# Folding a norm's channel factors into the two operations that split a weight, block by block

## The chip, the cores and the metric

The kernel runs on one core of a Trainium2 chip. The metric is the time of one execution in microseconds on the device. Engines are named as in the profile: PE is TensorE (PEld its weight loads), DVE is VectorE, ACT is ScalarE, POOL is GpSimd, and SP is SyncE, whose queue here issues all transfers between HBM and the core's memory.

## The reference

A trunk of two layers over 1024 positions and 1024 channels, float32 throughout. The first layer is a Conformer convolution: RMS norm, a projection to 3072 columns (two halves of a gated unit and an output gate), a causal depthwise convolution with 31 taps, layer norm, SiLU, gate, output projection, norm, residual. The second is differential attention with 8 heads over keys and values from the residual stream after the first layer. What matters here are its projections, each of which reads a normalised stream:

```python
def _rms_norm(x, g):
    y = xf * lax.rsqrt(jnp.mean(xf * xf, axis=-1, keepdims=True) + EPS)
    return (y * g.astype(jnp.float32)).astype(x.dtype)

kvh = _rms_norm(x, kv_g) @ w_kv        # keys and values, 2048 columns
h = _rms_norm(x, g_pre)
u = h @ w_in                           # queries and output gate, 2048 columns
```

The norm's factor per position is applied to a product after the matmul; its factor per channel, `kv_g` or `b_g_pre`, belongs to a row of the weight and can be multiplied into it.

## The kernel before, in words

**Products.** PE multiplies in a reduced float32 format. Every operand is therefore kept as a high part (the rounded value) and a low part (the rest), and each product is three matmuls: high by high, high by low, low by high (`THREE`). `act[t]` holds the split stream of one half of the positions (512 columns, t = 0 or 1), channels on the partitions, in eight blocks of 128 channels.

**Weights.** A weight piece is 128 output columns of a projection: a tile `wraw` of 128 partitions x 1024 elements, which are 8 channel blocks of 128 columns. `wprep` loads it (L564 is the line of every DMA), ACT rounds it into the high half of a tile `whl` (`R.copy`, L532) and DVE subtracts to give the low half (`R.tt`, L539). There are two `wraw` and three `whl` tiles (and one more, `whx`, for the first query piece). 32 of the pieces, those of the second layer's keys, values, queries and gate, carry a norm's channel factors: `wprep` gets them as `gain`. A value piece (`vproj`) is 4 channel blocks of 256 columns, two pieces for two heads; the other 24 (`zbproj`, `heads`) are 8 blocks of 128 columns. The factors lie in `pr` (`kv_g`, `b_g_pre`) or, for queries, in an 8-column tile `sm8`, which the profile lists as `sm`. In the kernel before, one DVE multiplication over the whole tile puts the factors into `wraw` in place ahead of the split.

**Stages.** The first layer (gated unit, convolution by DVE for four channel blocks and by PE for the other four, gate, layer norm, output projection, residual) fills about the first 430 us. Then the attention's heads follow, until about 960 us: for each head its weight pieces, projections (`pj`), scores (`s`, L1152), a softmax numerator (`e`: DVE L1161, then ACT L521), transposes (`t`, L1204), the split of the transposed weights (`at`: ACT L532, DVE L539), products with the values (`o`), and a norm over the head (`finish`). The next head's pieces are prepared while one head's attention runs. The output projection ends the kernel.

**Order.** Nothing runs in program order. The program records each instruction with its data dependences into a plan; `Plan.schedule` then simulates the five engines with a price in nanoseconds per instruction (`alts`), and puts every instruction at its place in its engine's queue, by a priority made of its place in the program, the longest chain behind it, constants (`TUNE`) and an offset for each labelled group (`OFFSETS`; "w" at a label's end is its weight piece, "cv0" the first channel block's convolution, "s23" the third pair of scores of head 3). Each engine then runs its queue in that order. An instruction whose input isn't there holds all behind it on that engine.

Of the kernel before, what the change touches and what calls it, by code (L numbers as in the profile page):

```python
# [12 lines left out]
AF = mybir.ActivationFunctionType  # L13
ALU = mybir.AluOpType
# [4 lines left out]
P = 128  # L19
# [111 lines left out]
class Op:  # L131
# [13 lines left out]

TUNE = dict(LOOK=2.2803,
           BG=19323277573972505648901158565292249389628248258332383962132468097051787264,
           FS=45301, FS0=1201, CS=0, EV=157158, WT=0.8342, CV0=46679, CV1=113660, WP=2955,  # L150
           ZS=-61794, PT0=8, PT1=8)

OFFSETS = {"": 20890, "w": 8673, "start1": -150, "x0": 332, "x1": 403, "x2": 60, "x3": 48533,
# [55 lines left out]


class Clock:
# [24 lines left out]
class Plan:  # L236
# [53 lines left out]
    def schedule(self):  # L290
# [16 lines left out]
        for o in self.ops:  # L307
            o.prio = max(o.seq + o.shift + OFFSETS.get(o.label, 0), min(o.seq, o.floor))
            o.prio = TUNE["WT"] * -tail[o] / 200.0 + (1 - TUNE["WT"]) * o.prio
            if o.early:  # L310
# [43 lines left out]
        while done < len(self.ops):  # L354
            best = None
            for e in engines:
# [22 lines left out]
                if pick is not None:  # L379
                    lim = s + TUNE["LOOK"] * dict(pick.alts)[e]  # L380
                    least = pick.prio - TUNE["BG"]
                    rush = [(t, o.prio, o) for t, o in cand
# [186 lines left out]
def trunk(ctx: ExitStack, tc, xT, wC, prm, wA, wAo, wK, wV, wB, wBo, wBo2, gpost, outT, out2):  # L569
# [3 lines left out]
    R = Plan(nc)  # L573
# [82 lines left out]
    f = lambda v: v.bitcast(F32)  # L656
# [8 lines left out]
    def wprep(src, gain=None, n_k=NT, k0=0, tag="whl", lo=("DVE",), parts=1):  # L665
        w = S // n_k
        sh, R.shift = R.shift, R.shift - TUNE["WP"]
        lb, R.label = R.label, R.label + "w"
        wl = "W" if R.lane in "BF" and tag == "whl" else R.lane
        hl = R.tile(tag, 2, n_k, w, lane=wl)  # L670
        raw = R.tile("wraw", n_k, w, lane=wl)
        n = n_k // parts
        for a in range(0, n_k, n):
            ks = slice(a, a + n)
            R.dma(raw[:, ks], src.rearrange("p (k c) -> p k c", c=w)[:, ks], 4 * P * S // parts,
                  R.gate)
            if gain is not None:
                g = gain[0][:, gain[1] + k0 : gain[1] + k0 + n_k].bc(2, [P, n_k, w])
                R.tt(raw.all(), raw.all(), g, ALU.mult)
            R.copy(hl[:, 0, ks], raw[:, ks])  # L680
            hl.done = R.tt(hl[:, 1, ks], raw[:, ks], f(hl[:, 0, ks]), ALU.subtract, lo)
        R.shift, R.label = sh, lb
        return hl
# [757 lines left out]
```

## Time and profile before

| what | value |
|---|---|
| runs shown, median | 1124.56 us (three runs, 1121.05 to 1125.19) |
| the profiled execution | 1127.16 us, span of its instructions 1125.4 us |
| mean granted clock of PE | 0.981 of full speed |
| busy: PE, DVE, ACT | 1074.9 us, 899.9 us, 445.6 us |

Busy times are sums of the instructions' durations, overlaps counted once. The span is from the first to the last instruction of the profiled execution; that execution lies 2.6 us above the median of the runs shown.

### The profile page before, as it was taken

The page shows a single profiled execution, that of the slowest core. Times are in us where ns is not written, and L with a number is a line of the kernel's source. Part 1 is how long each engine was busy: PE and PEld are TensorE (multiplying, and loading weights), DVE is VectorE, ACT ScalarE, POOL GpSimd, SP SyncE. Part 2 cuts the span into 40 slices and gives each one's busy share as a digit, 9 for nine tenths or more (in the row PEclk, how much of TensorE's full clock was granted, in tenths as well). Part 3 has the DMA queues.
Part 4 walks back from the last instruction along what each step waited for, and adds up shares of the span by engine and source line. Part 5 has one row for each costly group of instructions (what it writes and reads, how often), then busy time and mean ns, then how long its engine had stood idle before and what let it go on. Part 6 is the DMA issues. An engine that isn't in the chain of part 4 may idle for free.

```text
span 1125.4 us, 15385 instructions
## 1 busy us (share of the span) xinstructions
PE 1074.9 (96%) x5790; PEld 883.0 (78%) x5790; DVE 899.9 (80%) x1812; ACT 445.6 (40%) x824; POOL 4.8 (0%) x19
## 2 busy tenths in 40 slices
PE   7999899998999998999999999999999999999996
PEld 5788788886888886886888887988888888767874
DVE  7999969989895389938778778787886966878566
ACT  8112021125465354434345334454443443455421
POOL 0000000000000001000000000000000000000000
PEclk9999899998999999999999999999999999989998
DMA  9121541172112354441114121232121311731293
GB/s 339 63 75 57 169 150 65 48 244 55 57 38 73 100 169 146 168 169 38 38 63 145 58 75 38 76 131 75 58 75 58 113 57 38 262 106 60 96 328 141
DMA packets 52409, 121.31 MB, mean 108 GB/s; under 512 B 5488, under 2 KB 22128, under 8 KB 51184
## 3 DMA queue, kind: packets, MB, share of 16 engines
q1 hardware_dynamic: 52336, 120.34, 31.3%
q8 instruction: 45, 0.74, 0.3%
q14 instruction: 28, 0.23, 0.1%
HBM read 90.96 MB, written 29.36 MB: 107 GB/s over the span
## 4 chain that ended last, share of the span: by engine, by line
PE 79%; DVE 8%; DMA 7%; ACT 3%; issue 2%; SPq 1%; DVEq 0%; ACTq 0%
PE pj L498 45%; PE pjA L498 11%; PE pjB L498 6%; PE o L498 6%; PE s L1152 6%; PE t L1204 3%; DMA wc<-wC 2%; PE pjC L498 1%; DMA wraw<-wBo 1%; SPq L564 1%; DVE ya L559 1%; PE t L498 1%; DMA wraw<-wK 1%; ACT tmp L521 1%; DVE msum L539 1%
## 5 line engine op out<-in xcount | busy, mean ns | idle before, releaser
L498 PE MATMUL pj<-act,whl 128*128 128x512 f32 x1968 | 537.4, 405 | 7.0 <-ACT whl L532 5.7
L498 PEld LDWEIGHTS pj<-act,whl 128*128 128x128 f32 x1968 | 358.0, 191 | 87.5 <-ACT whl L532 5.9
L498 PE MATMUL pjA<-act,whl 128*128 128x512 f32 x672 | 186.8, 402 | 0.6 <-DVE whl L539 0.6
L532 ACT CAST whl<-wraw 128x1024 fp32r<-128x1024 f32 (+1 forms) x84 | 86.0, 1027 | 174.9 <-PE pj L498 114.9
L498 PEld LDWEIGHTS pjA<-act,whl 128*128 128x128 f32 x672 | 127.3, 191 | 32.0 <-DVE whl L539 1.0
L559 DVE SCALAR_TENSOR_TENSOR ya<-cc,pr,ya 128x1024 f32<-128x1024 f32 x116 | 148.7, 1282 | 2.4
L521 ACT ACTIVATE e<-e,sm 128x128 f32<-128x128 f32 (+7 forms) x128 | 99.3, 777 | 99.6 <-DVE sm L1161 61.8
L539 DVE TENSOR_TENSOR whl<-wraw,whl 128x1024 fp32r<-128x1024 f32 (+1 forms) x84 | 100.2, 1195 | 32.9 <-ACT whl L532 32.7
L498 PE MATMUL pj<-whl,act 128*128 128x256 f32 x768 | 112.2, 284 | 3.4 <-DVE tmp L559 3.4
L498 PEld LDWEIGHTS pj<-whl,act 128*128 128x128 f32 x768 | 100.7, 189 | 7.3 <-DVE tmp L559 4.3
L498 PE MATMUL o<-at,vt 128*128 128x256 f32 x480 | 100.5, 299 | 0.7 <-ACT at L532 0.7
L1161 DVE CUSTOM_DVE_ANT_0 e<-s,dist 128x128 f32<-128x128 f32 (+7 forms) x128 | 94.6, 752 | 6.6 <-PE s L1152 4.1
L498 PEld LDWEIGHTS o<-at,vt 128*128 128x128 f32 x480 | 78.3, 189 | 14.7 <-issue 4.4
L539 DVE TENSOR_TENSOR at<-t,at 128x512 fp32r<-128x512 f32 (+1 forms) x80 | 50.7, 634 | 33.4 <-ACT at L532 31.2
L1152 PE MATMUL s<-ks,qs 64*128 64x512 f32 (+2 forms) x576 | 73.1, 372 | 2.6 <-DVE sm L1161 2.5
L532 ACT CAST at<-t 128x512 fp32r<-128x512 f32 (+1 forms) x80 | 43.4, 543 | 78.6 <-PE t L1204 74.9
L1152 PEld LDWEIGHTS s<-ks,qs 64*128 64x128 f32 x576 | 48.5, 187 | 23.5 <-issue 8.1
L559 DVE SCALAR_TENSOR_TENSOR e<-e,sm,e 128x128 f32<-128x128 f32 (+3 forms) x64 | 52.2, 816 | 1.4
L1204 PE MATMUL t<-ident,e 128*128 128x128 f32 x288 | 50.4, 275 | 2.6 <-DVE og L539 1.7
L539 DVE TENSOR_TENSOR tmp<-pj,rn 128x512 f32<-128x512 f32 x48 | 32.9, 688 | 24.5 <-PE pj L498 20.7
L498 PE MATMUL pjB<-act,whl 128*128 128x512 f32 x192 | 52.3, 397 | 0.0
L498 PEld LDWEIGHTS pjB<-xq,wc 128*128 128x128 f32 x320 | 39.8, 200 | 8.3 <-issue 7.2
(177 smaller groups left out, 1078.0 us busy)
## 6 DMA issues: line engine op xcount, KB each, us to landing
wraw<-wA SPq DMA_DIRECT2D x22, 512.0 KB, 3.5
wc<-wC SPq DMA_DIRECT2D x8, 1280.0 KB, 8.7
wraw<-wAo SPq DMA_DIRECT2D x16, 512.0 KB, 3.6
wraw<-wB SPq DMA_DIRECT2D x16, 512.0 KB, 3.5
v_d<-tmp SPq DMA_DIRECT2D x32, 256.0 KB, 2.7
vt<-v_d SPq DMA_DIRECT2D x16, 512.0 KB, 3.3
wraw<-wBo SPq DMA_DIRECT2D x16, 512.0 KB, 4.3
go_d<-fx SPq DMA_DIRECT2D x12, 512.0 KB, 2.6
```

The source lines that it names most:

```text
L498: e.matmul(w[0], lhsT=r[2 * i], rhs=r[2 * i + 1], start=start and i == 0, stop=stop and i == k - 1)
L521: e.activation(w[0], r[0], func, **kw)
L532: (e.copy if hasattr(e, "activation") else e.tensor_copy)(w[0], r[0])
L539: lambda e, r, w: e.tensor_tensor(w[0], r[0], r[1], alu), [a, b], [out])
L559: e.scalar_tensor_tensor(w[0], r[0], s if imm else r[2], r[1], o1, o2)
L564: return self.op([("SP", 475.0)], lambda e, r, w: e.dma_start(w[0], r[0]), [src], [out], nbytes, gate)
L1152: en.matmul(w_[2 * (m // 6) + m % 2], lhsT=r[2 * m], rhs=r[2 * m + 1], start=m % 6 < 2, stop=m % 6 >= 4)
L1161: en.tensor_tensor_reduce(w_[0], r[0], r[1], -(0.5 ** (h + 1)), 3e38, ALU.add, ALU.min, w_[1])
L1204: R.op([("PE", 110.0)], lambda en, r, w: en.transpose(w[0], r[0], ident), [aw[qq][:, k0 : k0 + P]], [t_ps[:, i, :]])
```

## The change: what it does, and the diff

Where `wprep` gets channel factors, the multiplication over the whole tile, the rounding over the whole tile and the subtraction over the whole tile go. In their place each channel block gets two instructions: ACT copies the block times its factor (one number per partition, taken from memory as the instruction's scale) into the high half, and DVE computes block times factor minus high half (`R.stt`) into the low half. `wraw` is no longer written. The plan's prices are set to 370 ns and 310 ns for each block, whatever its width. Pieces without factors are prepared as before.

All constants of `TUNE` that are shown in the diff and nearly all of `OFFSETS` have other values as well, so that every engine's queue may have another order in all stages. Of the offsets a few stand here.

```diff
-TUNE = dict(LOOK=2.2803,
-           BG=19323277573972505648901158565292249389628248258332383962132468097051787264,
-           FS=45301, FS0=1201, CS=0, EV=157158, WT=0.8342, CV0=46679, CV1=113660, WP=2955,
+TUNE = dict(LOOK=4.0183,
+           BG=4782923213790355517589053156738505591805890650812152609421540987954733536182410412032,
+           FS=45301, FS0=1201, CS=0, EV=157158, WT=0.7858, CV0=46679, CV1=113660, WP=2955,
...
-           "x4": 9275, "x5": 3939, "x6": -3452, "x7": 989, "w0": 9002, "ab00": -15021, "ab10":
-           39455, "cv0": 379, "w1w": 3465, "ab11": 1145, "cv1": 13614, "w2": -413, "ab12": 7686,
+           "x5": 16654, "x6": -974, "x7": 937, "w0": -2620, "ab00": 1963, "ab10": 27502, "cv0":
+           -21992, "w1w": 9710, "ab01": 10765, "ab11": -17917, "cv1": 33686, "w2w": 1053, "w2":
...
             if gain is not None:
-                g = gain[0][:, gain[1] + k0 : gain[1] + k0 + n_k].bc(2, [P, n_k, w])
-                R.tt(raw.all(), raw.all(), g, ALU.mult)
+                for k in range(a, a + n):
+                    g = gain[0][:, gain[1] + k0 + k : gain[1] + k0 + k + 1]
+                    R.act(hl[:, 0, k], raw[:, k], AF.Copy, scale=g).alts = [("ACT", 370.0)]
+                    hl.done = R.stt(hl[:, 1, k], raw[:, k], g, f(hl[:, 0, k]), ALU.mult,
+                                    ALU.subtract)
+                    hl.done.alts = [("DVE", 310.0)]
+                continue
             R.copy(hl[:, 0, ks], raw[:, ks])
             hl.done = R.tt(hl[:, 1, ks], raw[:, ks], f(hl[:, 0, ks]), ALU.subtract, lo)
```

## Rows read from the trace of the kernel before

**Rows 1.** The page's first part: busy time, share of span, instructions by engine.

```profile
PE 1074.9 (96%) x5790; PEld 883.0 (78%) x5790; DVE 899.9 (80%) x1812; ACT 445.6 (40%) x824; POOL 4.8 (0%) x19
```

**Rows 2.** Busy time by stretch: start:end, length, engines, granted clock, DMA.

```profile
0.00:430.00 430.00, 409.44 (x1889) 333.03 (x1890) 363.35 (x492) 156.39 (x247) 1.77 (x17) 0.98 0.35 116
...
430.00:960.00 530.00, 518.31 (x3161) 432.08 (x3159) 416.42 (x1011) 225.12 (x462) 2.99 (x2) 0.99 0.24 82
...
960.00:1125.00 165.00, 147.11 (x746) 117.86 (x742) 120.13 (x310) 64.14 (x115) 0.00 (x0) 0.94 0.48 169
```

**Rows 3.** The chain of waits, 425 to 520 us: start, length, engine, tile, line.

```profile
430.90 1.24 DVE wraw L539
...
459.36 0.87 DVE wraw L539
...
499.14 8.26 DMA wraw<-wK
```

**Rows 4.** Two stretches of the attention's start, columns as in rows 2.

```profile
430.00:466.00 36.00, 29.92 (x175) 24.86 (x173) 34.08 (x70) 13.76 (x23) 2.99 (x2) 0.95 0.34 116
...
430.00:520.00 90.00, 80.89 (x457) 66.13 (x456) 65.22 (x145) 37.08 (x68) 2.99 (x2) 0.96 0.39 133
```

**Rows 5.** Instructions in order of time near 507 us: start, length, [idle before].

```profile
507.43 1.23 DVE L539 TENSOR_TENSOR wraw<-wraw,pr 128x1024 f32<-128x1024 f32 x1 [2.69 <-DMA wraw<-wK]
...
508.92 0.71 PE L1152 MATMUL s<-ks,qs 64*128 64x256 f32 x5 [2.02 <-DVE sm L1161]
```

**Rows 6.** Groups by shape: busy us, mean ns of one, idle before.

```profile
L532 ACT CAST whl<-wraw 128x1024 fp32r<-128x1024 f32 x80 | 83.6, 1048 | 174.9 <-PE pj L498 114.9 <-PE pjA L498 21.0 <-issue 19.5
...
L539 DVE TENSOR_TENSOR whl<-wraw,whl 128x1024 fp32r<-128x1024 f32 x80 | 97.5, 1220 | 32.6 <-ACT whl L532 32.4
...
L539 DVE TENSOR_TENSOR wraw<-wraw,pr 128x1024 f32<-128x1024 f32 x24 | 29.3, 1220 | 5.5 <-DMA wraw<-wK 3.0 <-DMA wraw<-wV 2.5
...
L539 DVE TENSOR_TENSOR wraw<-wraw,sm 128x1024 f32<-128x1024 f32 x8 | 9.7, 1218 | 3.2 <-DMA wraw<-wB 3.2
...
L559 DVE SCALAR_TENSOR_TENSOR tmp<-pj,rt,tmp 128x256 fp32r<-128x256 f32 x32 | 13.9, 478 | 6.5 <-ACT tmp L521 4.3 <-DMA x1t_d<-xr 2.2
...
L521 ACT ACTIVATE e<-e,sm 128x256 f32<-128x256 f32 x16 | 8.1, 506 | 7.3 <-DVE sm L1161 7.3
...
L521 ACT ACTIVATE e<-e,sm 128x128 f32<-128x128 f32 x16 | 6.4, 402 | 14.5 <-DVE sm L1161 10.0 <-DVE sm L539 3.1 <-DVE sm L559 1.2
...
L559 DVE SCALAR_TENSOR_TENSOR e<-e,sm,e 128x128 f32<-128x128 f32 x8 | 2.8, 350 | 0.1
```

**Rows 7.** Instructions in order of time, runs of equal ones merged.

```profile
403.61 2.36 DVE L539 TENSOR_TENSOR whl<-wraw,whl 128x1024 fp32r<-128x1024 f32 x2
...
512.10 0.35 DVE L559 SCALAR_TENSOR_TENSOR e<-e,sm,e 128x128 f32<-128x128 f32 x1
512.37 1.22 DVE L539 TENSOR_TENSOR whl<-wraw,whl 128x1024 fp32r<-128x1024 f32 x1
...
461.61 0.88 DVE L559 SCALAR_TENSOR_TENSOR tmp<-pj,rt,tmp 128x256 fp32r<-128x256 f32 x2
...
115.04 2.26 ACT L521 ACTIVATE yq<-pjB,pr 128x128 f32<-128x128 f32 x8 [2.49 <-PE pjB L498]
```

**Rows 8.** Who waited for whom, PE alone: us, times, longest.

```profile
PE pjB L498 <- DMA xq<-ca_d: 6.4, 2, 5.0
...
PE pjB L498 <- DVE msum L539: 5.2, 1, 5.2
...
PE o L498 <- ACT at L532: 0.7, 1, 0.7
...
PE pj L498 <- ACT whx L532: 0.3, 1, 0.3
```

**Rows 9.** Two joints of the first layer, columns as in rows 2.

```profile
116.00:136.00 20.00, 15.00 (x66) 11.90 (x65) 19.43 (x17) 1.30 (x5) 0.25 (x2) 0.95 0.71 224
258.00:276.00 18.00, 12.80 (x46) 9.22 (x45) 18.00 (x26) 9.30 (x12) 0.00 (x0) 0.81 0.17 59
```

More of the change, by code (lines that the diff above doesn't have):

```diff
@@ L144 @@
            ("SP", "POOL"): 940.0, ("SP", "SP"): 1000.0}
-TUNE = dict(LOOK=2.2803,
-           BG=19323277573972505648901158565292249389628248258332383962132468097051787264,
-           FS=45301, FS0=1201, CS=0, EV=157158, WT=0.8342, CV0=46679, CV1=113660, WP=2955,
+TUNE = dict(LOOK=4.0183,
+           BG=4782923213790355517589053156738505591805890650812152609421540987954733536182410412032,
+           FS=45301, FS0=1201, CS=0, EV=157158, WT=0.7858, CV0=46679, CV1=113660, WP=2955,
            ZS=-61794, PT0=8, PT1=8)
-OFFSETS = {"": 20890, "w": 8673, "start1": -150, "x0": 332, "x1": 403, "x2": 60, "x3": 48533,
[55 rows of a table removed]
+OFFSETS = {"": 16772, "w": -7524, "x0": 82, "x1": 4030, "x2": -487, "x3": 40816, "x4": 37792,
[56 rows of a table added]
 class Clock:
```

107 rows, old and new, of the table OFFSETS are left out of this document.

## The prediction

> **What bounds the kernel now.** I read the busy times first: PE is busy for 96% of the span, DVE 80%, ACT 40% [rows 1]. Such averages hide stages, so next the stretches. In the attention, where all 32 pieces with factors lie, PE is busy 518.3 of 530 us at a granted clock of 0.99, while DVE has 114 us and ACT 305 us to spare [rows 2]. PE bounds that stage, and the change takes no matmul away. All it can win there are PE's 11.7 idle us and what the clock lost beside them. The first layer holds another 20.6 idle us of PE and the tail 17.9 (430 − 409.4, 165 − 147.1) [rows 2], where no piece with factors is prepared; only the reordered queues can reach those.
>
> So where does the multiplication sit on the path? The chain of waits answers. From 430 to 471 us it runs almost wholly on DVE, and five factor multiplications are links of it, together 5.5 us; the first and the last of the five are in [rows 3]. DVE is busy 34.1 of 36 us there and PE only 29.9, with the clock at 0.95 [rows 4]: this is the one place of the attention where DVE sets the time. A sixth, near 507 us, is a link of another sort. It waited 2.69 us at DVE's head for a key piece (whose transfer is the chain's link at 499.14 [rows 3]); the softmax step behind it, whose scores had long been there, came late, and PE's next scores stood 2.02 us for it [rows 5]. Of PE's 11.7 idle us in the attention 9.1 lie ahead of 520 us [rows 2, 4]; after that it runs with next to no gap.
>
> **Step 1: DVE's work.** The tool here is the difference between a duration and a pitch. A whole-tile operation lasts 1.22 us [rows 6], but two in a row take 2.36 us, so the second starts 1.14 us after the first [rows 7]. Per piece the change removes a multiplication and a subtraction: 2 x 1.14 = 2.28 us of DVE. A 128-column block of the new kind is not in the trace as such; the nearest row is the softmax's combination of the same operation and width, 350 ns [rows 6], and the instruction behind it starts 0.27 us later [rows 7]. Eight make 2.16 us. For value pieces the 256-column form lasts 478 ns and two take 0.88 us, a pitch of 0.40 [rows 6, 7] (its source is in the matmul's accumulator, ours is not); four make 1.60. Sum by pitch: 24 x (2.16 − 2.28) + 8 x (1.60 − 2.28) = −2.9 − 5.4 = −8.3 us. By durations, if the blocks never overlap: 24 x (8 x 0.35 − 2.44) + 8 x (4 x 0.478 − 2.44) = 8.6 − 4.2 = +4.4 us. I take the pitch, since these blocks follow one another when ACT is ahead. So the fold hardly relieves DVE: it trades one long multiplication for eight fixed parts. "With no operation of its own" does not mean without its cost.
>
> [...]
>
> **Step 2: ACT's work.** Removed: a cast of 1048 ns, pitch about 0.95 (eight small ones take 2.26 us at 368 ns each, so about 0.10 us of each overlaps with the next [rows 7]). Added: eight blocks with a per-partition number. Nearest rows: the exponent over 128 columns 402 ns, over 256 columns 506 ns [rows 6], pitches 0.30 and 0.41. Sum: 24 x (2.4 − 0.95) + 8 x (1.64 − 0.95) = +40 us; by durations +60. Cover: ACT's 305 idle us of the attention's 530. Its share goes from 42% to 50%, or 54%. I take nothing for it. Without that cover it costs: see the burst below.
>
> **Step 3: the place on the path.** In 430 to 466 us six multiplications fall, four of them on 128-column pieces and two on value pieces. By pitch DVE gets 4 x 0.12 + 2 x 0.68 = 1.8 us shorter there, and DVE ends last. The ends: nothing gained up to the 5.5 us of the five links, if the blocks all slip off the chain. I take 1.8, because the blocks that replace them need nearly the same DVE time in a stretch that has 2 us of it left.
>
> **Step 4: who waits for the transfer.** The first instruction to touch a landed piece is now ACT's. DVE's stop near 507 us goes: the softmax step runs when its scores are there, and PE's 2.02 us with it. What is late next is ACT: the wait now stands at the head of its queue, and the exponents behind it wait. DVE's stops of this kind, this one among them, sum to 8.7 us [rows 6], 3.0 + 2.5 + 3.2, and I count only the one that PE felt. I take 2.0; the ends are 0 (ACT holds the exponent as long) and 3.8, if half of the 3.6 us that the clock took of 430 to 520 us (0.96 of 90 us [rows 4]) comes back too.
>
> **Step 5: finer readiness.** PE may start on a piece when its first block is split, about 0.75 us after ACT begins, instead of after three whole-tile steps of 3.5 us. PE's longest wait for a piece with factors was 0.3 us, for the first query piece [rows 8], so this is worth nothing while PE has other products to do, which is all of the attention after 520 us. The same holds for the tiles: pieces come free no later, and transfers start as they did.
>
> **Step 6: the new order.** Every queue may change. No row prices that. I take nothing and bound it by PE's idle stretches that it could close, or open again: two joints of the first layer, where PE stood 5.0 us (convolution input late [rows 8]) and 5.2 us (layer-norm mean late [rows 8]), with the clock at 0.95 of 20 us and 0.81 of 18 us [rows 9], worth 5.0 + 1.0 and 5.2 + 3.4, together 14.6.
>
> **Sum:** 1.8 + 2.0 = 3.8 us. Against the profiled execution's own 1127.16 us (1125.4 us span and 1.8 around it) this is 1123.4; that execution lies 2.6 above the median of the runs shown, so against the median: 1124.56 − 3.8 = **1120.8 us**.
>
> **Rivals.**
> - *The new order closes a joint.* The convolution's offset for the first channel block moves from 379 to −21992, which puts its loads and products earlier; the 116 us joint is just such a late input. For: 10.2 idle us lie there. Against: DVE is busy 19.4 of 20 and 18.0 of 18 us at the joints [rows 9], so an order can only shift what it does there. Half of 14.6: 7.3 more, 1113.5 us.
> - *The new order opens stops of the same kind.* PE idles only 50 us in the whole span, so there is more room to lose than to win. It ends slower than before from 9.4 us of new stops on (5.6 + 3.8); two joints' worth, 14.6, gives 1135.4 us.
> - *ACT's burst.* A piece now holds ACT for 2.4 us in a row instead of 0.95. If the split of the attention weights or an exponent queues behind it, PE stands. Today PE waits 0.7 us for that split [rows 8]. 32 pieces x 1.45 us = 46 us if all is exposed; a third gives 15.4 − 3.8 above before, 1136.2 us. It decides from a fifth on. Against: blocks are separate instructions and others can go between them.
> - *The blocks don't overlap.* If each DVE block waits for its ACT block, a piece takes DVE 8 x 0.402 = 3.2 us instead of 2.28, and a value piece 2.0; in the DVE-bound stretch that is 4 x 0.94 − 2 x 0.26 = +3.2, less the 2.0 of step 4: 1125.8 us. [...]
>
> **How the numbers follow.** About 0.5% (5.6 us) is what a measurement of this kernel tells from no change; the zone is 1118.9 to 1130.2. Forecast 0.42, with its own range 1117 to 1126 (of it 0.10 faster, 0.32 same). A joint closed 0.31 (0.30 faster). Stops opened 0.12 (0.11 slower). Burst 0.08 (0.07 slower). No overlap 0.07, all same. That makes faster 0.40, same 0.42, slower 0.18. The range must reach into the closed joint's case, to 1109, and to 1133 above, which leaves out some 0.05 below and 0.15 above.
>
> **What would show each step.** Right: 32 whole-tile multiplications fewer; 192 ACT and 192 DVE blocks of 128 columns and 32 of 256 each; DVE's block near 350 ns and 0.27 apart, its busy sum within −8 and +5 us; ACT's up by 40 to 60; no DVE wait on weight transfers in the attention; PE idle in 430 to 520 us down by some 4 us and elsewhere in the attention under 2. Wrong: PE's idle sums in the first layer or the tail change by more than the attention's (then the order made the time), PE waits on the attention-weight split above 3 us (burst), or DVE blocks 0.40 apart.

## The result and the profile after

The changed kernel takes 1110.7 us (median of four runs, 1109.9 to 1112.4) against 1124.0 us before (four runs): a ratio of 0.9883, interval 0.9864 to 0.9901, or 13 us faster. The profiled execution took 1110.67 us, with a span of 1108.9 us. The page's busy times, and the chain that ended last by engine (its second line):

```profile
PE 1068.4 (96%) x5790; PEld 878.3 (79%) x5790; DVE 889.6 (80%) x1972; ACT 482.8 (44%) x1016; POOL 3.8 (0%) x19
...
PE 84%; DVE 6%; DMA 4%; ACT 3%; issue 2%; SPq 1%; DVEq 0%; ACTq 0%
```

Against [rows 1] DVE lost 10.3 us, ACT gained 37.2, and PE, with the same 5790 instructions, was busy 6.5 us less. No matmul went, and the mean granted clock of this execution is 0.989 instead of 0.981, so a faster clock is the likely reason. The stretches that answer to [rows 2, 4, 9], and one of the attention's middle:

```profile
0.00:430.00 430.00, 413.18 (x1926) 335.80 (x1927) 369.58 (x516) 160.26 (x258) 2.57 (x18) 1.00 0.35 118
430.00:960.00 530.00, 522.33 (x3197) 436.21 (x3197) 411.90 (x1190) 263.80 (x657) 1.24 (x2) 0.99 0.25 86
960.00:1109.00 149.00, 132.92 (x669) 106.28 (x667) 108.13 (x268) 58.71 (x103) 0.00 (x0) 0.96 0.47 166
430.00:466.00 36.00, 33.93 (x205) 29.55 (x205) 31.77 (x77) 20.00 (x45) 1.24 (x2) 0.91 0.46 154
430.00:520.00 90.00, 86.53 (x510) 72.00 (x510) 67.99 (x184) 49.89 (x124) 1.24 (x2) 0.96 0.37 123
116.00:136.00 20.00, 20.00 (x109) 17.02 (x108) 19.50 (x16) 0.00 (x0) 0.12 (x1) 1.00 0.56 191
258.00:276.00 18.00, 14.42 (x60) 10.81 (x61) 17.67 (x29) 12.07 (x17) 0.00 (x0) 1.00 0.12 36
...
520.00:960.00 440.00, 435.80 (x2688) 364.21 (x2687) 343.91 (x1007) 213.91 (x534) 0.00 (x0) 1.00 0.23 79
```

The first layer's clock went from 0.98 to 1.00, the joint at 116 us is full of matmuls, and the one near 258 us is shorter and at full clock. But equal stretches of time don't hold equal work. A landmark does: the start of the first layer's last output product, the last start in the line of `pjB` that is fed by `whl`. First the kernel before, with the stretch up to that point, then the changed one:

```profile
L498 PE MATMUL pjB<-act,whl x192: 392/393/482, 347.4 to 436.2; 128*128 128x512 f32 x192
```

```profile
0.00:436.20 436.20, 415.64 (x1918) 338.08 (x1918) 368.51 (x505) 158.61 (x250) 1.77 (x17) 0.98 0.35 116
```

```profile
L499 PE MATMUL pjB<-act,whl x192: 390/394/482, 338.2 to 426.1; 128*128 128x512 f32 x192
```

```profile
0.00:426.10 426.10, 411.03 (x1917) 334.55 (x1918) 366.51 (x508) 158.69 (x253) 1.77 (x17) 1.00 0.35 118
```

The first layer, none of whose own pieces has factors, ends 10.1 us earlier, although the first value piece is now prepared ahead of that point (422 to 426 us; before, the first factor multiplication of any piece started at 430.9): PE idles 15.1 us instead of 20.6, and is busy 4.6 us less for the same products at the higher clock. What follows takes 682.8 us (1108.9 − 426.1) instead of 689.2. So of the profiled 16.5 us some 10 lie where the fold isn't.

The waits that answer to [rows 8], and ACT's own on transfers of pieces:

```profile
PE pjB L499 <- DMA xq<-ca_d: 3.1, 1, 3.1
PE pjB L499 <- DVE msum L540: 2.9, 1, 2.9
PE t L499 <- DVE dg L540: 1.7, 1, 1.7
...
PE o L499 <- ACT at L533: 0.7, 1, 0.7
...
ACT whl L522 <- DMA wraw<-wV: 4.7, 1, 4.7
...
ACT whl L522 <- DMA wraw<-wB: 1.9, 1, 1.9
```

How the first joint closed is to be read in the chain, 100 to 140 us. Before, a load of convolution weights is a link of it, and PE stands until the convolution's input follows on the same queue:

```profile
116.15 12.79 DMA wc<-wC
...
135.13 2.47 PE pjB L498 x10
```

After, the whole stretch of the chain is PE. It has projections until 131.4 us, and then runs the same convolution products without a stop:

```profile
127.36 2.10 PE pjA L499 x9
...
131.55 8.48 PE pjB L499 x76
```

The blocks themselves, by shape (columns as in [rows 6]):

```profile
L522 ACT ACTIVATE whl<-wraw,pr 128x128 fp32r<-128x128 f32 x128 | 40.9, 393 | 2.0 <-DMA wraw<-wB 1.9
...
L560 DVE SCALAR_TENSOR_TENSOR whl<-wraw,pr,whl 128x128 fp32r<-128x128 f32 x128 | 38.5, 345 | 0.0
...
L560 DVE SCALAR_TENSOR_TENSOR whl<-wraw,pr,whl 128x256 fp32r<-128x256 f32 x32 | 14.5, 477 | 2.3 <-ACT whl L522 2.3
L522 ACT ACTIVATE whl<-wraw,pr 128x256 fp32r<-128x256 f32 x32 | 14.2, 499 | 4.8 <-DMA wraw<-wV 4.7
```

And the chain where DVE had carried it [rows 3]. The first value piece's transfer, one ACT block and four DVE blocks are links of it, between the steps of a norm that end in `dg`; from 428 us on it is PE's for 20 us.

```profile
415.89 6.61 DMA wraw<-wV
422.52 0.52 ACT whl L522
423.07 0.48 DVE whl L560
...
426.98 1.24 DVE dg L540
...
428.26 0.73 PE t L499 x2
...
429.48 1.08 PE pj L499 x3
```

### The profile page after: what moved, and what is told of

It reads as the page before. It is cut to its first block, busy times and chain, and to the rows that moved or that the text cites. A ratio compares the mean times of both kernels' runs of the same rounds, so it can differ in the third digit from the quotient of the medians.

```text
span 1108.9 us, 15788 instructions
## 1 busy us (share of the span) xinstructions
PE 1068.4 (96%) x5790; PEld 878.3 (79%) x5790; DVE 889.6 (80%) x1972; ACT 482.8 (44%) x1016; POOL 3.8 (0%) x19
## 4 chain that ended last, share of the span: by engine, by line
PE 84%; DVE 6%; DMA 4%; ACT 3%; issue 2%; SPq 1%; DVEq 0%; ACTq 0%
PE pj L499 49%; PE pjA L499 11%; PE o L499 6%; PE pjB L499 6%; PE s L1158 6%; PE t L1210 3%; PE pjC L499 2%; DMA wc<-wC 1%; PE t L499 1%; DVE acc L540 1%; ACT tmp L522 1%; DMA xr<-xT 1%; DVE big L540 1%; DVE whl L540 1%; DMA wraw<-wV 1%
## 5 line engine op out<-in xcount | busy, mean ns | idle before, releaser
L499 PE MATMUL pj<-act,whl 128*128 128x512 f32 x1968 | 532.2, 403 | 10.8 <-ACT whl L533 5.7
L533 ACT CAST whl<-wraw 128x1024 fp32r<-128x1024 f32 (+1 forms) x53 | 53.6, 1016 | 129.2 <-PE pj L499 74.2
L1167 DVE CUSTOM_DVE_ANT_0 e<-s,dist 128x128 f32<-128x128 f32 (+7 forms) x128 | 94.6, 752 | 10.8 <-PE s L1158 7.7
L540 DVE TENSOR_TENSOR whl<-wraw,whl 128x1024 fp32r<-128x1024 f32 (+1 forms) x53 | 62.4, 1180 | 20.9 <-ACT whl L533 20.7
L1158 PE MATMUL s<-ks,qs 64*128 64x512 f32 (+2 forms) x576 | 70.8, 367 | 0.1
L522 ACT ACTIVATE whl<-wraw,pr 128x128 fp32r<-128x128 f32 (+1 forms) x160 | 55.1, 414 | 6.7 <-DMA wraw<-wV 4.7
L560 DVE SCALAR_TENSOR_TENSOR whl<-wraw,pr,whl 128x128 fp32r<-128x128 f32 (+1 forms) x160 | 53.0, 371 | 2.3 <-ACT whl L522 2.3
```

The lines of the kernel that those rows point to most:

```text
L499: e.matmul(w[0], lhsT=r[2 * i], rhs=r[2 * i + 1], start=start and i == 0, stop=stop and i == k - 1)
L522: e.activation(w[0], r[0], func, **kw)
L533: (e.copy if hasattr(e, "activation") else e.tensor_copy)(w[0], r[0])
L540: lambda e, r, w: e.tensor_tensor(w[0], r[0], r[1], alu), [a, b], [out])
L560: e.scalar_tensor_tensor(w[0], r[0], s if imm else r[2], r[1], o1, o2)
L1158: en.matmul(w_[2 * (m // 6) + m % 2], lhsT=r[2 * m], rhs=r[2 * m + 1], start=m % 6 < 2, stop=m % 6 >= 4)
```

## Experiments

Two theories stood at first. *Order*: the rewritten offsets made most of the gain, in the first layer, and the fold some 4 us. *Fold*: the fold made most of it. A rival for the fold's cost was the burst on ACT.

**1. The fold in the old order.** Every queue is that of the kernel before; the blocks stand in a row where the whole-tile cast and subtraction stood. (The queries' factor tile comes free at the place of the dropped multiplication, so some query pieces may use another head's factors.)

```diff
-                R.tt(raw.all(), raw.all(), g, ALU.mult)
-            R.copy(hl[:, 0, ks], raw[:, ks])
-            hl.done = R.tt(hl[:, 1, ks], raw[:, ks], f(hl[:, 0, ks]), ALU.subtract, lo)
+                R.tt(...).fn = lambda e, r, w: None
+                R.copy(hl[:, 0, ks], raw[:, ks]).fn = high      # n_k blocks on ACT
+                hl.done = R.tt(...); hl.done.fn = low           # n_k blocks on DVE
```

> The order of the kernel before on every engine; only the 32 pieces with factors are prepared the new way, their eight (or four) blocks in a row at the places of the whole-tile cast and subtraction, the multiplication gone. Theory 'order' (the new order of the first layer made most of the gain, the fold some 4 us between 430 and 520 us): 2 to 4 us faster than before, 1120 to 1122, the first layer's last output product starts near 436 us as before. Theory 'fold' (the fold made most of it): 1110 to 1114. Theory 'burst' (eight blocks in a row on ACT hold the softmax): slower than before, PE waits on the attention-weight split above 3 us.

Measured: 1133.2 us, ratio 1.0087 (1.0072 to 1.0102), 10 us slower. The first layer ends at 437.8, much as before, so the loss lies behind it: 696.2 us (span 1134.0) instead of 689.2. It comes late: from the landmark to the first split of attention weights this kernel takes 79.2 us (517.0 − 437.8), the kernel before 82.3 (518.5 − 436.2). In the attention's middle PE idles 8.2 us, where the whole attention before has 2.6 behind 520 us.

```profile
520.00:960.00 440.00, 431.85 (x2644) 358.55 (x2641) 339.61 (x972) 213.59 (x528) 0.00 (x0) 1.00 0.21 71
```

Theory *fold* falls. The 2 to 4 us that *order* gave the fold are there up to the first split (3.1 us) and are lost behind it. PE's wait on the attention-weight split is 1.2 us, so the burst does not act through that one wait. The chain of waits shows where it acts: from 520 to 1000 us, where no instruction of a piece is a link before, DVE's blocks now hold 4.6% of the chain and ACT's 2.2%, most of them in whole rows. Here a row on DVE holds a softmax step, and that the scores:

```profile
565.90 2.09 DVE whl L688 x8
567.99 0.20 DVE e L1175
...
568.25 0.62 PE s L1166 x5
```

So the rows on both engines cost time here, and DVE's hold more of the chain than ACT's.

**2. No fold in the new order.** The changed kernel's queues; multiplication and cast at a piece's first ACT block, subtraction at its first DVE block.

```diff
+                    h.fn = high if k == 0 else (lambda e, r, w: None)        # DVE mult, ACT cast
+                    hl.done.fn = low if k == 0 else (lambda e, r, w: None)   # whole subtraction
```

> The order of the changed kernel on PE, SP and all else; the 32 pieces are prepared the old way, multiplication and cast at the place of a piece's first ACT block, subtraction at the place of its first DVE block. Theory 'order': 2 to 6 us slower than the changed kernel, 1113 to 1117, first layer's last output product near 426 us. Theory 'fold': 1120 or more.

Measured: 1171.8 us, ratio 1.0439 (1.0413 to 1.0465). The first layer still ends at 427.0; all of the loss is behind it. It tells less than planned of the fold: the multiplication now stands in DVE's queue where the old kernel would not have put it.

**3 and 4. Only the constants exchanged**, with the plan free: the fold with the old `TUNE` and `OFFSETS`, and the old preparation with the new ones.

> The fold with the constants and offsets of the kernel before; the plan is free to move blocks. Theory 'order': first layer's last output product near 436 us, total 1118 to 1124. Theory 'fold': total 1110 to 1114, all of the gain behind 430 us.

> The new constants and offsets without the fold. Theory 'order': first layer's last output product near 426 us, total 1112 to 1118. Theory 'fold': total within 3 us of before.

Measured: 1145.7 us (1.0191, 1.0173 to 1.0210) and 1149.6 us (1.0225, 1.0206 to 1.0243). The landmark of the fold with the old constants, then of the old preparation with the new ones:

```profile
L498 PE MATMUL pjB<-act,whl x192: 392/398/482, 347.0 to 435.2; 128*128 128x512 f32 x192
```

```profile
L499 PE MATMUL pjB<-act,whl x192: 390/394/482, 337.3 to 425.5; 128*128 128x512 f32 x192
```

In all six kernels so far the first layer ends at 435 to 438 us with the old constants and at 425 to 427 with the new, fold or none. That half of *order* is shown. But as totals both expectations missed by over 20 us: constants made for one set of instructions gave a slow rest with the other. Behind the landmark the fold takes 709.3 us with the old constants (1144.5 − 435.2) and the old preparation 719.4 with the new ones (1144.9 − 425.5), where the changed kernel has 682.8 and the kernel before 689.2.

**5 and 6. The queues joined at the first layer's end.** Each engine's queue takes the first layer's instructions from one order and the rest from the other. Kernel 5 has no fold, the new first layer and the old rest; kernel 6 has the fold with its own order behind the old first layer.

```diff
+    place = [first[o] if o.seq < split else rest[o] + shift for o in ops]   # start times of two plans
+    # each engine issues strictly by place
```

(The kernels of runs 5, 6 and 9 carry a ready table of places; their diffs here say in one line how it was made.)

> No fold. Each engine's queue is joined from two: the first layer's instructions up to the second half's output products in the order of the new constants, all that follows in the order of the kernel before. If the first layer's order is worth its 10 us by itself: last output product of the first layer near 426 us instead of 436, the rest 689 us as before, a time of 1112 to 1117. If the attention gives the head start back: 1120 or more.

> With the fold. The other way round: the first layer in the order of the kernel before, all that follows in the order of the changed kernel. If the fold with the order fitted to it is worth the 6 us that the two traces show behind the first layer: last output product near 436 us, the rest 683 us, a time of 1116 to 1121. If it is worth nothing by itself: 1123 to 1127.

Measured: kernel 5 1117.3 us, ratio 0.9936 (0.9916 to 0.9955), 7.2 us faster than before; kernel 6 1121.5 us, ratio 0.9971 (0.9956 to 0.9987), 3.3 us faster. Together 10.5 of the 13.1 us; the rest, 2.6, is within the intervals (about 3 us for the sum). The landmarks are 429.0 and 433.5 us, 3 us off those expected, because the joint mixes the two orders around that point; so whole times are compared here. This is the measurement that divides the gain: of the 10.5 us about two thirds come with the first layer's order without any fold, about one third with the fold and the order that goes with it.

Not all of kernel 5's part lies in the first layer. By the traces 7.2 us of it come up to the landmark and 3.5 behind it (685.7 us instead of 689.2). There the stop at 507 us [rows 5] is missing, though the order of the pair on DVE is the old one. The multiplication waits 0.52 us instead of 2.69, and PE's next scores have no idle time:

```profile
497.85 1.22 DVE L735 TENSOR_TENSOR wraw<-wraw,pr 128x1024 f32<-128x1024 f32 x1 [0.52 <-DMA wraw<-wK]
...
499.10 0.85 PE L1348 MATMUL s<-ks,qs 64*128 64x256 f32 x6
```

The key piece was there 6.2 us after its transfer was issued (491.67 us), and not 8.3 us after (499.14) as in the profiled execution of the kernel before.

**7. ACT's blocks in a row, in the new order.**

```diff
+                    h.fn = row if k == 0 else (lambda e, r, w: None)   # all ACT blocks at the first's place
```

> The changed kernel with one difference: ACT does all blocks of a piece in a row at the first block's place. Theory 'burst' (a row of blocks on ACT holds the softmax; it made the loss of the fold in the old order): 5 to 8 us slower than the changed kernel, 1115 to 1119. Theory 'misfit' (that loss came from an order made for other instructions): within 2 us of the changed kernel.

Measured: 1120.3 us, ratio 0.9958 (0.9942 to 0.9973), 8 to 10 us slower than the changed kernel (0.0075 of 1124 us by ratios, 9.6 by medians). The same work in a row on ACT gives back more than the fold with its order had won, and as much as the fold had lost in the old order.

```profile
520.00:960.00 440.00, 431.64 (x2652) 359.53 (x2653) 341.26 (x1001) 210.81 (x528) 0.00 (x0) 1.00 0.22 73
```

PE idles 8.4 us there instead of 4.2. ACT's blocks are now 3.3% of the chain from 520 to 1000 us; in the changed kernel they are not among the lines that the view lists. Here the split of attention weights stands behind a row:

```profile
692.80 2.35 ACT whl L683 x8
...
695.63 0.48 ACT at L533
...
696.15 0.51 PE o L499 x2
```

The burst is real. In the changed kernel only 8 of the 24 pieces with 128-column blocks have all eight in one unbroken row in ACT's queue.

**8. One more whole-tile operation per piece on DVE**, ahead of the first block, its result overwritten.

```diff
+                    if k == 0:
+                        hl.done.fn = more    # tensor_tensor over the whole tile, then the block
```

> The changed kernel with one whole-tile multiplication more per piece on DVE, ahead of the piece's first DVE block, its result overwritten by the blocks: 32 x 1.14 = 36 us of DVE work. If DVE's work on the pieces is covered by PE, as the sum of the prediction has it outside 430 to 466 us: 1 to 5 us slower than the changed kernel, 1112 to 1116. If DVE's time is what the fold sold: 15 us or more slower.

Measured: 1138.8 us, ratio 1.0126 (1.0108 to 1.0144), 28 us slower than the changed kernel for 36 us of work (DVE's busy time is up by 37.0). The added multiplications are links of the chain from 520 to 1000 us, 4.3% of it.

**9. The stop at 507 us alone.** The kernel before with one pair on DVE exchanged.

```diff
+    place[factor_multiplication] = place[softmax_step] + 1
```

> The kernel before with one pair on DVE exchanged and nothing else: the factor multiplication that stood 2.69 us for its transfer at 507 us now comes behind the softmax step that it held. If step 4 of the prediction is right: PE's wait of 2.02 us is gone and the time falls by 2.0 to 3.8 us, 1120 to 1122. If the next thing is late in its place: within 1 us of before.

Measured: 1124.15 us, ratio 0.9991 (0.9975 to 1.0007): 1 us, and 0 is not excluded, nor are the 2.0 expected. The trace does show what the step claimed: the multiplication still waits, but the softmax step is done, and PE's next scores have no idle time.

```profile
504.17 0.28 DVE L1356 CUSTOM_DVE_ANT_0 e<-s,dist 128x128 f32<-128x128 f32 x1
...
505.69 1.23 DVE L734 TENSOR_TENSOR wraw<-wraw,pr 128x1024 f32<-128x1024 f32 x1 [1.23 <-DMA wraw<-wK]
...
506.02 0.61 PE L1347 MATMUL s<-ks,qs 64*128 64x256 f32 x6
```

**10. Each ACT block done twice.**

```diff
+                    h.fn = lambda e, r, w: [e.activation(...) for _ in range(2)]
```

> The changed kernel with each ACT block of a piece done twice: some 40 us of ACT work more, at the blocks' own places. If ACT's idle time covers it, as step 2 of the prediction takes it: at most 3 us slower than the changed kernel, 1111 to 1114. If what stands behind a block on ACT is what counts, as the row of blocks showed: 8 us or more slower.

Measured: 1160.7 us, ratio 1.0317 (1.0285 to 1.0348), 50 us slower than the changed kernel. ACT's added work is 89 us (571.8 instead of 482.8 us busy) and not the 40 of the expectation: that was the net of step 2, with the cast taken off, while here the whole blocks are doubled. ACT still idles 200 of the 530 us from 430 to 960 us, but its blocks are 20.5% of the chain from 520 to 1000 us. The page's busy times, and the wait on the attention-weight split, 10.8 us instead of 0.7:

```profile
PE 1084.0 (94%) x5790; PEld 883.6 (76%) x5790; DVE 900.1 (78%) x1972; ACT 571.8 (49%) x1240; POOL 3.8 (0%) x19
...
PE o L499 <- ACT at L533: 10.8, 12, 1.8
```

**11. A quarter of the low halves on POOL**, in two instructions each, as an attempt at a better kernel.

```diff
+                    if k >= n - n // 4:      # POOL: raw *= g; low = raw - high
+                        hl.done.fn = pool
```

> The changed kernel with the low halves of each piece's last quarter of blocks (56 of 224, some 16 us of DVE work) made by POOL, which is idle, in two instructions each. If DVE's work is worth what the added multiplication cost per us (28 us for 36): 5 to 12 us faster than the changed kernel, 1099 to 1106. If POOL is too slow or slows DVE beside it: slower than the changed kernel.

Measured: 1116.2 us, ratio 0.9928 (0.9899 to 0.9956), 5 us slower than the changed kernel, with intervals that just overlap. POOL needs 0.86 + 0.54 us for what DVE does in 0.35, and DVE's busy time falls by only 5.2 us (889.6 to 884.4) for 56 blocks fewer; its remaining 128-column blocks with `pr` took 372 ns instead of 345:

```profile
L687 POOL TENSOR_SCALAR wraw<-wraw,pr 128x128 f32<-128x128 f32 x32 | 27.4, 857 | 206.9 <-ACT whl L522 163.3 <-PE pj L499 43.4
L688 POOL TENSOR_TENSOR whl<-wraw,whl 128x128 fp32r<-128x128 f32 x46 | 24.9, 542 | 3.8
```

**12. A quarter of DVE's blocks left out**, to see whether less DVE work is worth anything.

```diff
+                    if tag == "whl" and k >= n - n // 4:
+                        hl.done.fn = lambda e, r, w: None
```

> The changed kernel without the low halves of each piece's last quarter of blocks (54 of 224, so the products there use stale low parts): some 16 us of DVE work less, nothing in its place. If each us of DVE's work on the pieces costs time in either direction (28 us for 36 added): 8 to 12 us faster than the changed kernel, 1099 to 1103. If the added work only came late in a full queue, and DVE has slack where the blocks lie: within 3 us of the changed kernel, 1108 to 1112.

Measured: 1111.0 us, ratio 0.9890 (0.9868 to 0.9913), the changed kernel's time, with 13.7 us less of DVE work (889.6 to 875.9 us). So kernel 8 did not show that DVE bounds the attention. Leaving out the last blocks of each piece is worth nothing, work put ahead of the first block costs 0.77 us per us: DVE has slack, but not ahead of the instructions that PE waits for next. (The two differ in place as well as in sign; the same place was not tried both ways.)

## Why the prediction was right or wrong

The direction was right and the time lay in the range, but the likeliest case, 1120.8 us, was not what happened. The measured gain is 13 us where 3.8 were summed.

**The step that failed is step 6**, the new order, of which the text took nothing; and with it the choice of the likeliest case. What happened is the rival that a joint of the first layer closes (0.31, 1113.5 us), and a little more. Its mechanism is in the trace as it was named: the stop of 5.0 us at 116 us is gone, that near 258 us is 2.9 us instead of 5.2, and the clock at both is 1.00 instead of 0.95 and 0.81. The wait on a later convolution input, near 238 us, grew from 1.4 to 3.1 us. PE's idle time fell by 10.0 us in all (50.5 to 40.5), 5.5 of them up to the landmark and so more than in the attention, which is one of the signs of being wrong that the prediction had named. Kernel 5 gives the first layer's order, with nothing else changed, 7.2 us; the rival's price was 7.3. That the two agree is partly luck: the price was half of 14.6 by choice, and by the traces a third of kernel 5's gain lies behind the first layer. The weak point in the text was to see that both joints were reachable by the diff, to price them, and still to hold an unpriced order for neutral.

**Step 1, DVE's work: right in size, and rightly given no price of its own.** Block durations 345 and 477 ns (350 and 478 taken), DVE's busy time down 10.3 us (8.3 by pitch, and a little outside the −8 to +5 that were named as a sign). The sum went by pitch, and a DVE total that fell by 10.3 us instead of rising by 4.4 agrees with that. A block of an eighth of the elements took 345 ns where the whole tile took 1220 [rows 6], so eight blocks are 2.76 us by their durations against 2.44 for the two operations they replace. But in the changed kernel's trace three blocks in a row took 0.87 us (438.68 us) and eight 2.19 us (480.58 us), 0.26 apart at 345 ns each, so some 0.08 us of each overlapped with the next one. Kernel 12 shows the cover: 13.7 us less of DVE work changes nothing.

**Step 2, ACT's work: right in size (+37 us, 40 taken), wrong in its cover.** Idle time of an engine was no cover here for work that stood in front of something in its queue: kernel 10 pays 50 us for 89 more of such work. In the changed kernel, where most blocks lie between other ACT instructions, hardly any is a link of the chain behind 520 us; gathered in a row the same blocks cost 8 to 10 us (kernel 7). That is the burst rival, which had 0.08. As an account of the changed kernel it was rightly small, since its counter-argument (others can go between) held. The fold in the old order, with rows on both engines, costs 10 us as well (kernel 1). There ACT's rows are a part of the loss and DVE's, which the rival did not name, the larger part of the chain; how the 10 us divide between them was not tried.

**Steps 3 and 4, together 3.8 us:** kernel 6, the fold with its own order behind the old first layer, measured 3.3 us (1.5 to 4.9). The sum came out near but its parts did not, so that is partly luck. Up to the first scores the changed kernel wins 0.7 us from the landmark on (503.7 − 436.2 against 492.9 − 426.1), where step 3 had 1.8. From the first scores to the first split of attention weights it wins 5.0, where step 4 had 2.0. The first starts of both, before, after, and in kernel 9:

```profile
L1152 PE MATMUL s<-ks,qs x576: 271/386/792, 503.7 to 1022.3; 64*128 64x512 f32 x96, 64*128 64x256 f32 x64, 64*128 64x384 f32 x32
...
L532 ACT CAST at<-t x80: 459/582/598, 518.5 to 1053.3; 128x512 fp32r<-128x512 f32 x48, 128x384 fp32r<-128x384 f32 x32
```

```profile
L1158 PE MATMUL s<-ks,qs x576: 271/386/502, 492.9 to 1007.2; 64*128 64x512 f32 x97, 64*128 64x256 f32 x63, 64*128 64x384 f32 x32
...
L533 ACT CAST at<-t x80: 455/585/597, 502.7 to 1038.1; 128x512 fp32r<-128x512 f32 x48, 128x384 fp32r<-128x384 f32 x32
```

```profile
L1347 PE MATMUL s<-ks,qs x576: 271/386/792, 503.2 to 1018.0; 64*128 64x512 f32 x97, 64*128 64x256 f32 x63, 64*128 64x384 f32 x32
...
L727 ACT CAST at<-t x80: 458/582/597, 514.1 to 1049.1; 128x512 fp32r<-128x512 f32 x48, 128x384 fp32r<-128x384 f32 x32
```

In kernel 9's trace, with two DVE instructions exchanged, 3.9 of those 5.0 us are gone (14.8 to 10.9 us), but its timed gain is 1 us with an interval that reaches from −0.8 to 2.8. The trace has a reason. The key piece came 6.8 us after its issue (498.93 to 505.69) and not 8.3, so a part of the 3.9 is the transfer's. In the old order, with this transfer, the softmax step would have come 1.14 us after 505.69 and the scores some 1 us later than they did; that is an estimate, and it fits the timed gain. Kernel 5 closes the stop with neither fold nor exchange (11.2 us between the two starts, 496.2 to 507.4). So the mechanism is shown, a step held behind a multiplication that waits; its length of 2.0 us was seen in one execution only, and it takes no fold to close it.

The other part of step 4, what is late next, is seen too: DVE has no wait on a piece's transfer any more, and ACT has two, 4.7 and 1.9 us. The longer one is on the chain shown above: DVE waited 2.3 us for ACT's first block, the norm's steps behind it came late, and PE stood 1.7 us for `dg`. Before, PE had stood 2.3 us for the same tile.

**Step 5, finer readiness,** was given nothing and not tried by itself. The rival *no overlap* did not come: DVE's blocks are 0.35 us long, and it waited 3.2 us in all for ACT's.

**What stays open:** the 2.6 us that kernels 5 and 6 leave of the gain, and how the 3.3 us divide between the fold and the order behind the first layer. Each order that was run is made for one of the two kinds of preparation, and the other kind in it is slower (kernels 1 to 4). No order neutral to both was run, so the fold has no value of its own that these runs could state.

## What to carry to other kernels

Where a change comes with a rewritten order, price the order first: list the stops of the engine that bounds the kernel in all stages, also those the edit's own code doesn't reach, with the clock beside them. Here the stop of 5.0 us at 116 us went and that of 5.2 us near 258 us fell to 2.9, and the granted clock of those stretches rose from 0.95 and 0.81 to 1.00.

In these runs idle time on an engine covered added work only as far as the order put it in the gaps. Add work at the places in question before counting on a low busy share: here ACT at 50% and DVE at 78% of the attention had little room at those places (50 us lost for 89 us of added ACT work in kernel 10, 28 for 36 of DVE's in kernel 8), though taking 13.7 us of DVE's work away gained nothing (kernel 12).

One profile is one execution. The stop at 507 us hung on a single transfer, which took 8.3 us in the profile before, 6.8 us in kernel 9's and 6.2 us in kernel 5's; so time the kernel without such a stop before counting on its length.

To divide a gain between an edit and its order, join the queues of both kernels at a stage border, and use a landmark of equal work instead of equal times.

## What the runs showed of the hardware

The clock was worth nearly as much as the idle time: in the first layer PE was busy 4.6 us less for the same products, at a granted clock of 1.00 instead of 0.98, next to 5.5 us of idle time saved. The old first-layer order showed 0.98 in four further executions (kernels 1, 3, 6 and 9, first 420 us) and the new one 0.99 or 1.00 in eight (kernels 2, 4, 5, 7, 8 and 10 to 12), so it goes with the order and not with the execution.
